# Operands of products 4 and 3 behind products 6 and 4, modulation streams split in turn, put-aside results fetched into the second weight ring

## The chip, the cores and the metric

The kernel runs on one core of a Trainium2 chip. The metric is the time of one execution on the device in microseconds (us). A core has five engines with instruction streams of their own: PE (matrix products), DVE (elementwise on vectors), ACT (elementwise with functions, and casts), POOL (elementwise) and SP (here it issues transfers only). An engine runs its instructions in order, and engines wait for one another by semaphores.

## The reference

One layer of a diffusion transformer over 1024 latent tokens and 256 context tokens of width 1024: a SwiGLU feed-forward half step (hidden width 2816), a mixer (a gated short convolution and attention with 8 query and 2 key heads, merged by gates), a second feed-forward half step and a last norm. Each of the three parts begins with an RMS norm whose result is shifted and scaled, and ends with a gate; shift, scale and gate come from the condition `c` through `w_mod` (1024 x 9216). The functions around which the change turns:

```python
def rms_norm(x, g):
    xf = x.astype(jnp.float32)
    y = xf * lax.rsqrt(jnp.mean(xf * xf, axis=-1, keepdims=True) + EPS)
    return (y * g.astype(jnp.float32)).astype(x.dtype)

def modulate(h, shift, scale):
    return h * (1.0 + scale) + shift

def swiglu(h, w_in, w_out):
    a, b = jnp.split(h @ w_in, 2, axis=-1)
    return (jax.nn.silu(a) * b) @ w_out
...
def conv_branch(bg, cg, vc, conv_w):
    return bg * short_conv(cg * vc, conv_w)
...
def merge_branches(y_conv, o_attn, gate_logits, w_bc, w_ba, w_out):
    g_conv, g_attn = jnp.split(jax.nn.sigmoid(gate_logits), 2, axis=-1)
    return (g_conv * (y_conv @ w_bc) + g_attn * (o_attn @ w_ba)) @ w_out
```

The layer calls `modulate(rms_norm(x, g), shift, scale)` before each part, multiplies by `w_in` (or the mixer's `w_in` of width 6656), and adds `gate * result` to the stream.

## The kernel before

**Arithmetic.** Each fp32 operand is split into a high part, rounded to the matrix engine's fp32r, and a low part, the remainder; a product is three matmuls (high·high, high·low, low·high). `split` does it: the cast to the high part is ACT's, the subtraction for the low part DVE's.

**Products.** The large projections use a Winograd form of the 2 x 2 block product: seven products 1 to 7 instead of eight, for a pair of weight column blocks `(a, b)` of 128 columns each. Left operands are weights or sums of weights (`s1`, `s2`, `s3`, which POOL makes from the raw weights in `lefts`); each is split into a tile `wl` of a ring of four. Right operands are the normed tokens or sums of them, `r1` to `r7`, each in four tiles of 128 rows (k = 0 to 3), made once for a whole projection by `norm0` and `norm1` and kept. A product is four k times three matmuls of 128 x 512. `Winograd.first`, `second` and `third` run the products 1, 2, then 6, 7, 4, then 5, 3, and DVE adds their results in `u`, `c`, `v` and `b`.

**Before the norm of the second half of tokens is there.** Products 1 and 2 need only the first half of the tokens. `start` (lines 664 and following) runs them for the first `n_ahead` pairs while `norm1` makes `r5`, `r6` and at last `r7`, `r4` and `r3` (`late`); it keeps the results `u` and `c` of two pairs on the chip, in a tile `uc` of the ring `wh` (the second weight ring, four slots), and puts those of the others aside in device memory (`put_aside`, tiles `ucd`). `fetch` brings them back, one pair ahead. By the end of `start` all of `norm1` has been run in the program's order (`r7` with the sixth pair, `r4` with the seventh, `r3` with the eighth of nine), so the calls of `late` in `second` find nothing to do. In the first feed-forward the same stands in the loop over `start_together`.

**Rings.** Short-lived tiles (`ttile`) share a pool of eleven slots: `s1` to `s3`, `u`, `c`, `v`, `b`, `y`, the modulation's `rawm` (a loaded piece of `w_mod`), `macc` (its running sums, one for each stream), `acch`, `accl` and `mrow`.

**Modulation.** What is not needed at the start is worked out beside the projections by generators of small steps (`later_mod`): eight steps load a piece of `w_mod` each and add it, times a column of `silu(c)`, to one or two sums on DVE; then the sums are split, PE adds over the partitions, and four small transfers turn the row to columns. `all_later_mods` is run in the first feed-forward's loop, `STEPS[j]` steps at the end of iteration j; m = 6 to 8 (`late_steps`) beside the mixer's projections and the second feed-forward.

**The second matrix of a feed-forward.** `row_products` runs the products in the order 2, 1, 4, 6, 5, 7, 3 over the hidden rows, in groups of two rows. When a product ends, its four banks are added into the stream by DVE (`add`, with the gate), and `after` puts out finished rows or begins the next norm.

**Order.** A scheduler places the instructions of each engine by what they wait for, save those issued while `strict` is set, which keep the order of the program. So the code's order decides only in part, and the rows below are read from the built programs. Line 88 is the helper through which every instruction is issued, so the profile gives it for all of them, and one goes by the tiles' names.

Of the kernel before, what the change touches and what calls it, by code (L numbers as in the profile page):

```python
# [41 lines left out]
STEPS = (0, 4, 4, 4, 5, 5, 5, 5, 5, 5, 5, 2, 12)  # L42
WAIT = 4
# [6 lines left out]
def tile_dit_layer(  # L50
# [211 lines left out]
    def later_mod(m, halves=(0, 1), streams=None):  # L262
# [3 lines left out]
        for half in halves:  # L266
# [12 lines left out]
            for _ in range(WAIT):  # L279
                yield  # L280
            parts = []
            for acc in accs:
                ah, al = ttile("acch", dt=F32R), ttile("accl", dt=F32R)
                split(acc, ah, al)
                parts.append((ah, al))
            for _ in range(6):
                yield
            for (ah, al), v in zip(parts, streams):
                mod, pm = (modl, modc)[v], ps_t()
                matmul(pm[:1], ones_r[:], ah, start=True, stop=False, pinned=True)  # L290
                matmul(pm[:1], ones_r[:], al, start=False, stop=True, pinned=True)
                row = ttile("mrow")
                act.copy(out=row[:1], in_=pm[:1])
                mcol = small("mcol", 4)
                for j in range(4):
                    sp.dma_start(out=mcol[:, j : j + 1], in_=row[:1, j * P : (j + 1) * P])
                c0 = m * 8 + half * 4
                dve.tensor_add(out=mod[:, c0 : c0 + 4], in0=mcol[:], in1=bcol[:, c0 : c0 + 4])
            yield
# [166 lines left out]
    class Winograd:  # L466
# [194 lines left out]
        def start(self, norm):  # L661

            for i in range(self.n_ahead):
                t = wpool.tile([P, 2, 512], F32, tag="wh", name=uniq("uc"), bufs=W_BUFS)
                u, c = t[:, 0], t[:, 1]
                act.copy(out=u, in_=self.product(1))
                run(norm, 2 if i == 0 else 1)
                dve.tensor_add(out=c, in0=u, in1=self.product(2))
                if i < RESIDENT:
                    self.started.append((u, c))  # L670
                else:
                    self.put_aside(t)
            run(norm, 9 - self.n_ahead)
            self.prefetch(4)
            self.late = norm
# [51 lines left out]
        def fetch(self):  # L727

            if self.started and not isinstance(self.started[0], tuple):
                u, c = ttile("u"), ttile("c")  # L730
                for i, t in enumerate((u, c)):
                    load(t, self.started[0][:, i])
                self.started[0] = u, c
# [9 lines left out]
        def second(self, u):  # L743
# [3 lines left out]
            run(self.late, 4)  # L747
# [4 lines left out]
            run(self.late)  # L752
            return v, b

# [40 lines left out]
    def row_products(w, rows, add, after=lambda i, k: None, halves=False):  # L795
# [113 lines left out]
        chain = None  # L909
        for i in (2, 1, 4, 6, 5, 7) + (() if halves else (3,)):  # L910
# [3 lines left out]
            for g, (k, m) in enumerate(groups):  # L914
# [5 lines left out]
                sums(i, g)  # L920
                strict[0] = False
                after(i, k)
            for o, ch in to[i]:
                for d in range(4):
                    add(o + d, ch, ps[d])
            after(i, rows.n)
        if halves:
            kept = []
            ps = [ps_s(256) for _ in range(4)]
            for k, m in groups:  # L930
                for lr in operands(3, k, m):
                    step(3, ps, len(kept), *lr, n=256)
                    kept.append(lr)
                after(8, k)
# [173 lines left out]
    for i in range(7):  # L1108
        if i == 3:
            tx = fetch_tokens(CC)  # L1110
        run(norm1, 1)
# [10 lines left out]
    run(norm1, 1)  # L1122
# [107 lines left out]
    for j in range(NH):  # L1230
        half1.side = side(j) if j >= SIDE_FROM else None
        if j > SIDE_FROM and j % 2:
            raws = context_rows(j)
        u, c = half1.next_first()
        v, b = half1.second(u)
        spill(c, b, j, C0)
        spill(*half1.third(u, v), j, C1)
        run(steps, STEPS[min(j, len(STEPS) - 1)])
        if j == SIDE_FROM - 1:
            for i in range(SIDE_FROM):  # L1240
# [5 lines left out]
                run(steps, 3)  # L1246
# [48 lines left out]
    def after1(i, k):  # L1295
# [23 lines left out]
        if i == 3 and k in (0, 4):  # L1319
# [24 lines left out]
    for i in range(KD):  # L1344
# [4 lines left out]
        if i > 1:  # L1349
            run(late_steps, 5)  # L1350
        for ch, bg, gc in mixed():
            if i > 1:
                run(late_steps, 4)
# [488 lines left out]
    for j in range(NH):  # L1842
        if j > 1:
            run(late_steps, 3)
        u, c = fast.next_first()
        v, b = fast.second(u)
        spill(c, b, j, C0)
        spill(*fast.third(u, v), j, C1)
# [77 lines left out]
```

## Time and profile before

| | us |
|---|---|
| median of 3 runs (lowest to highest) | 2686.76 (2683.47 to 2690.48) |
| the profiled execution's own time | 2688.7 |
| its span | 2686.9 |
| PE busy in it | 2643.4 |
| DVE busy in it | 2007.1 |
| ACT busy in it | 1166.1 |

By time of the span: the first feed-forward's first matrix to about 690 us (from about 277 us the side products of the context tokens stand among it), its second matrix to about 938, the mixer's projections from there to about 1250, attention, the merge, and the second feed-forward from about 2010 to the end. Most windows of 67 us have PE busy throughout. Read such a profile by looking for the windows where it isn't, then for what ended the idle time there, then one engine further back.

### The profile page before, as it was taken

The page shows a single profiled execution, that of the slowest core. Times are in us where ns is not written, and L with a number is a line of the kernel's source. Part 1 is how long each engine was busy: PE and PEld are TensorE (multiplying, and loading weights), DVE is VectorE, ACT ScalarE, POOL GpSimd, SP SyncE. Part 2 cuts the span into 40 slices and gives each one's busy share as a digit, 9 for nine tenths or more (in the row PEclk, how much of TensorE's full clock was granted, in tenths as well). Part 3 has the DMA queues.
Part 4 walks back from the last instruction along what each step waited for, and adds up shares of the span by engine and source line. Part 5 has one row for each costly group of instructions (what it writes and reads, how often), then busy time and mean ns, then how long its engine had stood idle before and what let it go on. Part 6 is the DMA issues. An engine that isn't in the chain of part 4 may idle for free.

```text
span 2686.9 us, 37399 instructions
## 1 busy us (share of the span) xinstructions
PE 2643.4 (98%) x13593; PEld 2236.0 (83%) x13593; DVE 2007.1 (75%) x3356; ACT 1166.1 (43%) x2317; POOL 521.3 (19%) x409
## 2 busy tenths in 40 slices
PE   8999999999999999999999999999999999999998
PEld 5788898888788877888999888877888888888888
DVE  5888888786887889877488666775458875667875
ACT  6633543333454632333244666674236333334543
POOL 1244012121110044232033111000001533230200
PEclk9999999999999999999999999999999999999998
DMA  7655653346973445433213211002524543228731
GB/s 267 236 180 166 223 184 124 109 130 240 293 169 102 149 137 165 134 114 116 97 48 103 95 62 49 24 25 78 167 85 146 184 145 99 83 90 305 165 83 63
DMA packets 369920, 364.84 MB, mean 136 GB/s; under 512 B 27830, under 2 KB 261448, under 8 KB 369736
## 3 DMA queue, kind: packets, MB, share of 16 engines
q1 hardware_dynamic: 360712, 345.17, 39.0%
q0 software_dynamic: 9024, 17.30, 4.0%
q8 instruction: 106, 1.74, 0.3%
q14 instruction: 78, 0.64, 0.1%
HBM read 296.30 MB, written 66.06 MB: 135 GB/s over the span
## 4 chain that ended last, share of the span: by engine, by line
PE 88%; DVE 6%; DMA 2%; ACT 2%; issue 1%; SPq 1%; POOL 0%; DVEq 0%; ACTq 0%; POOLq 0%
PE ps L88 73%; PE po L88 7%; PE pt L88 7%; DMA rawm<-in_w_mod_dram 1%; DVE macc L88 1%; DVE wl L88 1%; SPq L88 1%; DVE xb L88 0%; DVE r L88 0%; ACT r L88 0%; DMA raw<-in_ffn_w_in_dram 0%; DMA xtok<-in_ctx_dram 0%; DVE ol L88 0%; DVE x L88 0%; DVE pts L88 0%
## 5 line engine op out<-in xcount | busy, mean ns | idle before, releaser
L88 PE MATMUL ps<-r,wl 128*128 128x512 f32 x5232 | 1213.4, 392 | 11.6 <-ACT wl L88 6.8
L88 PEld LDWEIGHTS ps<-r,wl 128*128 128x128 f32 x5232 | 983.9, 189 | 220.0 <-ACT wl L88 9.0
L88 ACT CAST wl<-s 128x512 fp32r<-128x512 f32 x256 | 158.0, 620 | 338.3 <-PE ps L88 266.6
L88 POOL TENSOR_TENSOR s<-raw 128x512 f32<-128x512 f32 x64 | 92.4, 1444 | 993.8 <-PE ps L88 346.6
L88 ACT CAST wl<-raw 128x512 fp32r<-128x512 f32 x286 | 176.4, 619 | 250.0 <-PE ps L88 160.6
L88 DVE TENSOR_TENSOR wl<-raw,wl 128x512 fp32r<-128x512 f32 x284 | 202.6, 717 | 68.3 <-ACT wl L88 64.7
L88 DVE TENSOR_TENSOR wl<-s,wl 128x512 fp32r<-128x512 f32 x256 | 231.8, 906 | 12.3 <-ACT wl L88 10.7
L88 POOL TENSOR_TENSOR s<-raw,s 128x512 f32<-128x512 f32 x64 | 99.8, 1560 | 363.9 <-DVE wl L88 354.4
L88 DVE SCALAR_TENSOR_TENSOR macc<-rawm,silu_c,macc 128x512 f32<-128x512 f32 x168 | 137.9, 837 | 9.5 <-DMA rawm<-in_w_mod_dram 9.1
L88 PE MATMUL ps<-wh,r 128*128 128x256 f32 x768 | 141.6, 285 | 0.0
L88 DVE TENSOR_TENSOR pts<-pt,pts 128x512 fp32r<-128x512 f32 x160 | 108.8, 687 | 39.4 <-ACT pts L88 38.4
L88 DVE TENSOR_TENSOR u<-u,ps 128x512 f32<-128x512 f32 x168 | 114.2, 680 | 28.5 <-PE ps L88 28.4
L88 DVE TENSOR_REDUCE m<-ps 128x1 f32<-128x512 f32 (+1 forms) x192 | 110.9, 596 | 31.0 <-PE ps L88 30.3
L88 ACT CAST pts<-pt 128x512 fp32r<-128x512 f32 x160 | 93.2, 593 | 88.7 <-PE pt L88 86.8
L88 ACT CAST rh<-hid 128x512 fp32r<-128x512 f32 x132 | 81.6, 621 | 112.2 <-PE ps L88 96.2
L88 PE MATMUL ps<-rh,wl 128*128 128x512 f32 x360 | 122.0, 389 | 0.0
L88 PEld LDWEIGHTS ps<-wh,r 128*128 128x128 f32 x768 | 120.6, 192 | 0.0
L88 ACT CAST wh<-raw 128x512 fp32r<-128x512 f32 (+1 forms) x88 | 69.3, 795 | 103.0 <-PE ps L88 79.5
L88 PE MATMUL po<-pts,vh 128*128 128x512 f32 x256 | 110.5, 437 | 1.5 <-ACT pts L88 1.5
L88 DVE TENSOR_TENSOR rl<-hid,rh 128x512 fp32r<-128x512 f32 x132 | 90.1, 686 | 26.5 <-ACT rh L88 13.5
L88 PE MATMUL ps<-wl,r 128*128 128x256 f32 x384 | 108.8, 283 | 0.0
L88 PE MATMUL ps<-kl,qs 128*128 128x512 f32 x384 | 105.3, 397 | 0.0
(298 smaller groups left out, 5068.1 us busy)
## 6 DMA issues: line engine op xcount, KB each, us to landing
raw<-in_ffn_w_in_dram SPq DMA_DIRECT2D x125, 512.0 KB
raw<-in_ffn_w_out_dram SPq DMA_DIRECT2D x72, 512.0 KB
rawm<-in_w_mod_dram SPq DMA_DIRECT2D x128, 256.0 KB
raw<-in_w_in_dram SPq DMA_DIRECT2D x61, 512.0 KB
hid<-hd SPq DMA_DIRECT2D x40, 512.0 KB
ws<-in_ffn_w_out_dram POOLq DMA_DIRECT2D x30, 512.0 KB, 6.6
ucd<-uc SPq DMA_DIRECT2D x22, 512.0 KB
hd<-c SPq DMA_DIRECT2D x38, 256.0 KB
```

The lines of the kernel that those rows point to most:

```text
L88: inst = getattr(self.engine, name)(*args, **kw)
```

## The change

It makes five edits. (1) The late operands: `r4` is now made behind product 6 of the first pair and `r3` behind product 4, in the program's order, where both were made in `start`; `r7` stays there, at the last pair but one. (2) A modulation sum is split and added over the partitions one stream after the other, without the waiting steps between, so that half a matrix takes 12 steps in place of 19 (two streams); the steps an iteration are fewer and, in the feed-forwards, spread over it. (3) A fetched pair lands in one tile of the ring `wh`, by one transfer of 512 KB, in place of two tiles of the eleven slots. (4) In `row_products` a product's results are added behind the first group of the next product, in the program's order. (5) The first steps of the mixer's norm stand at groups 2 and 6 of the last product in place of 0 and 4.

```diff
-STEPS = (0, 4, 4, 4, 5, 5, 5, 5, 5, 5, 5, 2, 12)
-WAIT = 4
+STEPS = (0, 3, 3, 3, 3, 3, 3, 4, 4, 4, 4, 1, 8)
...
     def later_mod(m, halves=(0, 1), streams=None):
...
-            for _ in range(WAIT):
-                yield
-            parts = []
-            for acc in accs:
+            for acc, v in zip(accs, streams):
                 ah, al = ttile("acch", dt=F32R), ttile("accl", dt=F32R)
                 split(acc, ah, al)
-                parts.append((ah, al))
-            for _ in range(6):
                 yield
-            for (ah, al), v in zip(parts, streams):
                 mod, pm = (modl, modc)[v], ps_t()
...
                 dve.tensor_add(out=mod[:, c0 : c0 + 4], in0=mcol[:], in1=bcol[:, c0 : c0 + 4])
-            yield
+                yield
...
     def start(self, norm):
...
-                run(norm, 2 if i == 0 else 1)
+                run(norm, 2 if i == 0 else 1 if i < 5 or i == self.n_ahead - 2 else 0)
...
-            run(norm, 9 - self.n_ahead)
             self.prefetch(4)
             self.late = norm
...
     def fetch(self):
 
             if self.started and not isinstance(self.started[0], tuple):
-                u, c = ttile("u"), ttile("c")
-                for i, t in enumerate((u, c)):
-                    load(t, self.started[0][:, i])
-                self.started[0] = u, c
+                t = wpool.tile([P, 2, 512], F32, tag="wh", name=uniq("uc"), bufs=W_BUFS)
+                load(t[:], self.started[0][:])
+                self.started[0] = t[:, 0], t[:, 1]
...
     def second(self, u):
 
             v, b = ttile("v"), ttile("b")
             dve.tensor_add(out=u, in0=u, in1=self.product(6))
-            run(self.late, 4)
+            self.late_operands(1)
             dve.tensor_add(out=v, in0=u, in1=self.product(7))
             if self.side:
                 self.side(0, self.left())
             dve.tensor_sub(out=b, in0=v, in1=self.product(4))
-            run(self.late)
+            self.late_operands()
             return v, b
+
+        def late_operands(self, n=None):
+            strict[0] = True
+            run(self.late, n)
+            strict[0] = False
...
     def row_products(w, rows, add, after=lambda i, k: None, halves=False):
...
-        chain = None
+        chain, results = None, []
+
+        def add_results():
+            while results:
+                i, ps = results.pop()
+                for o, ch in to[i]:
+                    for d in range(4):
+                        add(o + d, ch, ps[d])
+                after(i, rows.n)
...
                 sums(i, g)
+                add_results()
                 strict[0] = False
                 after(i, k)
-            for o, ch in to[i]:
-                for d in range(4):
-                    add(o + d, ch, ps[d])
-            after(i, rows.n)
+            results.append((i, ps))
+        if not halves:
+            add_results()
...
                     kept.append(lr)
+                add_results()
                 after(8, k)
...
     for i in range(7):
         if i == 3:
             tx = fetch_tokens(CC)
-        run(norm1, 1)
+        run(norm1, 1 if i < 4 or i == 6 else 0)
         run(start, 2)
...
     run(start)
-    run(norm1, 1)
     half1.late = norm1
...
+        n_steps = STEPS[min(j, len(STEPS) - 1)]
         u, c = half1.next_first()
+        run(steps, n_steps // 3)
         v, b = half1.second(u)
         spill(c, b, j, C0)
+        run(steps, n_steps // 3)
         spill(*half1.third(u, v), j, C1)
-        run(steps, STEPS[min(j, len(STEPS) - 1)])
+        run(steps, n_steps - n_steps // 3 * 2)
...
-                run(steps, 3)
+                run(steps, 2)
...
-        if i == 3 and k in (0, 4):
+        if i == 3 and k in (2, 6):
             run(norms2, 1)
...
         if i > 1:
-            run(late_steps, 5)
+            run(late_steps, 3)
         for ch, bg, gc in mixed():
             if i > 1:
-                run(late_steps, 4)
+                run(late_steps, 2)
...
     for j in range(NH):
-        if j > 1:
-            run(late_steps, 3)
+        n_steps = j > 1
         u, c = fast.next_first()
+        run(late_steps, n_steps)
         v, b = fast.second(u)
         spill(c, b, j, C0)
+        run(late_steps, n_steps)
         spill(*fast.third(u, v), j, C1)
```

The number of matmuls, sums and casts is the same; SP issues 22 transfers fewer.

ACT at the start of the mixer's projections. `r7`, `r4` and `r3` are right operands, `wl` tiles are weight parts, each made by its cast (the first four `wl` are those of products 6, 7, 4 and 5 of the first pair), `uc` is the result of product 1. Before:

```order
L88 CAST r7_1526_8821<-t34_1511_8756 128x512
L88 CAST r4_1534_8863<-t34_1473_8587 128x512
L88 CAST r4_1535_8866<-t34_1485_8642 128x512
L88 CAST r4_1536_8869<-t34_1498_8699 128x512
L88 COPY uc_1557_8955<-ps_1559_8959 128x512
L88 CAST r4_1537_8872<-t34_1511_8756 128x512
L88 CAST r3_1545_8914<-h12_1472_8586 128x512
L88 CAST r3_1546_8917<-h12_1484_8641 128x512
L88 CAST r3_1547_8920<-h12_1497_8698 128x512
L88 CAST r3_1548_8923<-h12_1510_8755 128x512
L88 CAST wl_1554_8936<-s2_1552_8931 128x512
L88 CAST wl_1558_8956<-s3_1553_8932 128x512
```

and now:

```order
L87 CAST r7_1532_8883<-t34_1503_8740 128x512
L87 COPY uc_1541_8915<-ps_1543_8919 128x512
L87 CAST wl_1538_8896<-s2_1536_8891 128x512
L87 CAST wl_1542_8916<-s3_1537_8892 128x512
L87 CAST wl_1544_8933<-raw_1534_8888 128x512
L87 CAST wl_1547_8952<-s1_1535_8890 128x512
L87 CAST r4_1558_8980<-t34_1465_8571 128x512
L87 CAST r4_1559_8983<-t34_1477_8626 128x512
L87 CAST r4_1560_8986<-t34_1490_8683 128x512
L87 CAST r4_1561_8989<-t34_1503_8740 128x512
L87 CAST wl_1562_8993<-s2_1536_8891 128x512
L87 CAST wl_1569_9020<-s2_1567_9015 128x512
```

The casts of `r4` and `r3` stood ahead of the first weight part; now four weight parts stand ahead of `r4`, and two more ahead of `r3`.

DVE at the end of product 2 of the first feed-forward's second matrix. The `x1` rows add that product's four banks to the stream, `wl` and `wh` are low halves of the weights of product 1 (`wl_1186` is its first before, `wl_1178` now), `rl` low halves of hidden rows, `hid` sums of them. Before:

```order
L88 TENSOR_TENSOR hid_1104_6558<-hid_1105_6559,hid_1104_6558 128x1024
L88 SCALAR_TENSOR_TENSOR x1_1159_6794<-ps_1126_6582,gate1_l_6554,x1_1159_6794 128x512
L88 SCALAR_TENSOR_TENSOR x1_1160_6796<-ps_1127_6583,gate1_l_6554,x1_1160_6796 128x512
L88 SCALAR_TENSOR_TENSOR x1_1161_6798<-ps_1128_6584,gate1_l_6554,x1_1161_6798 128x512
L88 SCALAR_TENSOR_TENSOR x1_1162_6800<-ps_1129_6585,gate1_l_6554,x1_1162_6800 128x512
L88 TENSOR_TENSOR hid_1106_6560<-hid_1106_6560,hid_1104_6558 128x1024
L88 TENSOR_TENSOR rl_1203_7015<-hid_1112_6566,rh_1202_7014 128x512
L88 TENSOR_TENSOR wl_1186_6920<-raw_1185_6918,wl_1186_6920 128x512
L88 TENSOR_TENSOR wh_1189_6941<-raw_1185_6918,wh_1189_6941 128x512
```

and now:

```order
L87 TENSOR_TENSOR rl_1195_6999<-hid_1104_6550,rh_1194_6998 128x512
L87 SCALAR_TENSOR_TENSOR x1_1151_6778<-ps_1118_6566,gate1_l_6538,x1_1151_6778 128x512
L87 SCALAR_TENSOR_TENSOR x1_1152_6780<-ps_1119_6567,gate1_l_6538,x1_1152_6780 128x512
L87 TENSOR_TENSOR wl_1178_6900<-raw_1177_6898,wl_1178_6900 128x512
L87 SCALAR_TENSOR_TENSOR x1_1153_6782<-ps_1120_6568,gate1_l_6538,x1_1153_6782 128x512
L87 SCALAR_TENSOR_TENSOR x1_1154_6784<-ps_1121_6569,gate1_l_6538,x1_1154_6784 128x512
L87 TENSOR_TENSOR wh_1181_6921<-raw_1177_6898,wh_1181_6921 128x512
L87 TENSOR_TENSOR hid_1098_6544<-hid_1098_6544,hid_1096_6542 128x1024
```

The first weight part of product 1 stood behind four `x1` rows, a `hid` and an `rl`; now it stands behind two `x1` rows.

ACT in the first feed-forward, at a fetch. `uc_380` is a fetched tile of the ring `wh`, `c_361` a fetched tile of the eleven slots; the row is its Silu. Before, with the next four weight parts:

```order
L88 ACTIVATE u_313_1574<-u_313_1574 128x512
L88 CAST wl_366_1841<-s2_345_1733 128x512
L88 ACTIVATE c_361_1818<-c_361_1818 128x512
L88 CAST wl_373_1868<-s2_371_1863 128x512
L88 CAST wl_375_1888<-s3_372_1864 128x512
L88 CAST wl_377_1906<-raw_369_1860 128x512
L88 CAST wl_388_1947<-s1_370_1862 128x512
```

and now:

```order
L87 CAST wl_344_1726<-s2_327_1631 128x512
L87 ACTIVATE uc_380_1933<-uc_380_1933 128x512
L87 CAST wl_351_1753<-s2_349_1748 128x512
L87 CAST wl_354_1776<-s3_350_1749 128x512
L87 CAST wl_356_1794<-raw_347_1745 128x512
L87 CAST wl_363_1824<-s1_348_1747 128x512
```

In both a Silu of a fetched tile stands ahead of weight parts. SP, which issues the transfers, has around that fetch now:

```order
L87 DMA raw_347_1745<-in_ffn1_w_in_dram 128x8x128
L87 DMA raw_367_1859<-in_ffn1_w_in_dram 128x8x128
L87 DMA hd_1088<-uc_292_1459 128x512
L87 DMA uc_380_1933<-ucd_184_912 128x1024
L87 DMA rawm_353_1773<-in_w_mod_dram 128x512
L87 DMA rawm_358_1814<-in_w_mod_dram 128x512
L87 DMA rawm_360_1819<-in_w_mod_dram 128x512
L87 DMA hd_1088<-uc_314_1576 128x512
```

The `hd` rows store results; the second store of `uc_292` stands directly ahead of the fetch of `uc_380`, and loads of `w_mod` stand behind it.

## The prediction

> **What bounds the kernel now.** I read the busy shares first, then what PE waited for, then the windows.
>
> ```profile
> span 2686.9 us, 37399 instructions
> PE 2643.4 (98%) x13593; PEld 2236.0 (83%) x13593; DVE 2007.1 (75%) x3356; ACT 1166.1 (43%) x2317; POOL 521.3 (19%) x409
> ```
>
> PE is busy for 2643.4 of 2686.9 us: 43.5 us are idle, and only that, with what a halved clock adds, can be won while PE's work stays as it is. The change adds and removes no matmul. DVE holds 75% on average and is the next engine.
>
> ```profile
> PE ps L88 <- ACT wl L88: 8.0, 4, 5.1
> PE ps L88 <- DVE wl L88: 3.0, 3, 1.8
> ...
> PE pt L88 <- DVE wl L88: 1.7, 1, 1.7
> ...
> PE pt L88 <- ACT wl L88: 1.4, 1, 1.4
> ```
>
> In the view of PE's waits (total, times, longest) the dearest releaser is `wl`, a split weight part: the high half is an ACT cast, the low half a DVE subtraction. 8.0 + 3.0 + 1.7 + 1.4 = 14.1 us over nine waits. The windows say where.
>
> ```profile
> 938.00:1005.00 67.00, 61.95 (x264) 50.70 (x263) 59.42 (x99) 25.76 (x49) 28.15 (x17) 0.95 0.41 134
> 1005.00:1072.00 67.00, 64.43 (x271) 52.39 (x270) 62.45 (x91) 19.14 (x35) 27.32 (x19) 0.95 0.54 172
> 1072.00:1139.00 67.00, 67.00 (x297) 54.99 (x296) 54.75 (x82) 23.80 (x41) 19.08 (x13) 1.00 0.41 126
> 268.00:335.00 67.00, 63.87 (x478) 60.11 (x477) 56.89 (x103) 34.73 (x68) 0.00 (x0) 1.00 0.71 226
> 670.00:737.00 67.00, 63.58 (x293) 52.40 (x293) 59.05 (x84) 31.15 (x53) 8.40 (x7) 1.00 0.95 293
> ```
>
> A row is length, busy time of PE, PEld, DVE, ACT and POOL, then the granted clock (1.00 is full). 1072–1139 is undisturbed: 297 matmuls in 67 us, 0.226 us each, so a product of 12 takes 2.7 us. The four disturbed windows lose 5.05, 2.57, 3.13 and 3.42 us of busy time, and two also lose clock:
>
> ```profile
> 942.40:949.30 6.90, 5.74 (x14) 4.48 (x15) 5.83 (x10) 2.67 (x6) 2.79 (x1) 0.52 0.25 89
> 1058.50:1065.40 6.90, 5.92 (x14) 4.67 (x15) 6.69 (x11) 2.28 (x4) 2.32 (x3) 0.52 0.55 171
> ```
>
> Here PE is busy for 5.74 and 5.92 us at about half the clock, so about 2.9 and 3.0 us are lost beside the idle time.
>
> **Step 1, late operands behind products 6 and 4 (start of the mixers, 938 us).**
>
> ```profile
> 936.17 3.74 ACT L88 CAST r<-t 128x512 fp32r<-128x512 f32 x7
> ...
> 940.82 2.18 ACT L88 CAST r<-h 128x512 fp32r<-128x512 f32 x4
> 942.89 1.14 ACT L88 CAST wl<-s 128x512 fp32r<-128x512 f32 x2
> ...
> 937.93 4.29 DVE L88 TENSOR_TENSOR r<-t,r 128x512 fp32r<-128x512 f32 x7
> ...
> 943.57 6.68 PE L88 MATMUL ps<-r,wl 128*128 128x512 f32 x16 [5.05 <-ACT wl L88]
> ```
>
> ACT writes eight casts of r4 and r3 at about 0.52 us before the first weight part of product 6; DVE does eight subtractions at about 0.6 us (4.29 over 7). The change puts those of r4 behind product 6 and of r3 behind product 4, so the first cast of `wl` comes 8 × 0.52 = 4.2 us earlier, at 938.7, and PE starts 0.68 us later as now, at 939.4: 0.9 us idle in place of 5.05. PE then does four matmuls with high halves (0.9 us) and asks for the low half of product 6, whose subtraction follows r7's four (to 940.3) and the sum of `uc`: ready at 941.6, so 1.3 us more. Behind that, product 3 wants r3, which now stands behind two more weight casts, and the next pair's raw weights; by the same counting about 1.2 us. So 3.4 us of idle time stay of 5.05, and the 2.9 us of clock go if these gaps don't trip the gate again: a gain of 4.5, or 2.8 with one more half-clock window of 3.4 us (cost 1.7). [...] Bounds: 8.0 (all gone) and 0 (the raw weights come no earlier, PE merely waits later).
>
> What trips the gate, the trace shows:
>
> ```profile
> 97.07 0.33 PE L88 MATMUL pt<-ident,xtok 128*128 128x128 f32 x1 [0.61 <-DMA xtok<-in_ctx_dram]
> ...
> 98.94 1.56 PE L88 MATMUL ps<-r,wl 128*128 128x512 f32 x4 [1.32 <-ACT uc L88]
> ...
> 99.40:102.80 3.40, 3.40 (x10) 2.67 (x9) 2.87 (x3) 3.40 (x7) 3.32 (x3) 0.53 0.02 6
> ```
>
> Between 96 and 99.4 us PE stood 0.61 + 1.32 = 1.9 us, and the next 3.4 us ran at half clock. The window 670–737 lost 3.42 us in waits of under 2 us each (the two large ones stand in step 3) and kept 1.00.
>
> [...]
>
> **Step 2, modulation streams in turn, `u` and `c` in the other ring (1055 us).**
>
> ```profile
> 1057.01 0.62 ACT L88 CAST wl<-s 128x512 fp32r<-128x512 f32 x1 [6.41 <-POOL s L88]
> ...
> 1053.04 1.47 POOL L88 TENSOR_TENSOR s<-raw 128x512 f32<-128x512 f32 x1 [10.38 <-DVE accl L88]
> 1055.60 1.37 POOL L88 TENSOR_TENSOR s<-s,raw 128x512 f32<-128x512 f32 x1 [1.09 <-DMA yd<-y]
> ...
> 1057.68 0.73 PE L88 MATMUL ps<-r,wl 128*128 128x512 f32 x2 [1.51 <-ACT wl L88]
> 1059.48 2.07 PE L88 MATMUL ps<-r,wl 128*128 128x512 f32 x4 [1.07 <-DVE wl L88]
> ```
>
> POOL's weight sum waited 10.38 us, and what ended it was the subtraction of `accl`: a slot of the ring of 11 that `s1`, `s2`, `s3`, `u`, `c`, `v`, `b`, `y` and the modulation's tiles share. The second sum waited on the store of a `y`, the same ring. The change takes two of the eleven away for a put-aside pair and splits each stream where it ends, so the waits that held the high and low halves through six further steps are gone. I count the whole stall: 1.51 + 1.07 + 3.0 = **5.5**. Bounds: 0, if another tile of the ring is the last one there, and 5.5.
>
> **Step 3, results added behind the next product's first group (701 us).**
>
> ```profile
> 701.81 2.72 DVE L88 SCALAR_TENSOR_TENSOR x<-ps,gate_l,x 128x512 f32<-128x512 f32 x4
> 702.44 0.62 ACT L88 CAST wl<-raw 128x512 fp32r<-128x512 f32 x1 [0.29 <-DMA raw<-in_ffn_w_out_dram]
> ...
> 703.11 0.50 PE L88 MATMUL pt<-rh,wl 128*128 128x512 f32 x1 [1.39 <-ACT wl L88]
> ...
> 706.18 0.68 DVE L88 TENSOR_TENSOR wl<-raw,wl 128x512 fp32r<-128x512 f32 x1
> ...
> 706.92 0.73 PE L88 MATMUL pt<-rh,wl 128*128 128x512 f32 x2 [1.67 <-DVE wl L88]
> ```
>
> The low half came at 706.18 behind four gated sums (2.72 us), a sum of `hid` and an `rl`. In the new order it stands behind two sums: 703.1, before PE asks for it at 705.2. The 1.67 us go; the 1.39 us end with a load and stay. Gain **1.7**, bounds 0 and 3.1. No other product of this stage shows such a wait, so the same edit there gives nothing.
>
> **Step 4, fewer modulation operations ahead of the side products (277–287 us).**
>
> ```profile
> 272.91 1.14 ACT L88 CAST wo<-raw 128x512 fp32r<-128x512 f32 x2 [5.06 <-DMA raw<-in_ffn_w_out_dram]
> ...
> 277.32 0.39 PE L88 MATMUL ps<-h1ch,wl 128*128 128x256 f32 x1 [1.13 <-ACT wl L88]
> ...
> 285.37 1.41 DVE L88 SCALAR_TENSOR_TENSOR macc<-rawm,silu_c,macc 128x512 f32<-128x512 f32 x2
> 286.69 1.28 DVE L88 TENSOR_TENSOR wl<-raw,wl 128x512 fp32r<-128x512 f32 x2
> 287.43 0.51 PE L88 MATMUL ps<-h1ch,wl 128*128 128x256 f32 x2 [1.80 <-DVE wl L88]
> ```
>
> Fewer steps an iteration (3 for 5) and a share of them earlier in it take the `macc` pairs (1.41 us) from ahead of `wl`; `wo` is loaded earlier, so its casts no longer hold ACT for 5.06 us before the first `wl`. Of 1.13 + 1.80 = 2.9 us I take **2.5**; bounds 0 and 2.9.
>
> **Step 5, the fetch itself and the norms.** Twenty-two transfers of 512 KB replace 44 of 256 KB: the same bytes. The cost is a wait. The ring has four slots, so the fetch can be issued only when the second store of the pair before has landed, and in ACT's order the Silu of the fetched `uc` stands ahead of four weight casts. Something like it is there now:
>
> ```profile
> L88 SPq DMA_DIRECT2D c<-ucd x22: 319/377/486, 151.5 to 2173.8; - x22
> ...
>   ACT c L88: 40.4, 13
> ...
> 200.23 0.42 SPq L88 DMA_DIRECT2D u<-ucd  x1
> ...
> 205.01 0.63 ACT L88 ACTIVATE c<-c 128x512 f32<-128x512 f32 x1 [6.17 <-DMA c<-ucd]
> ```
>
> ACT waited 40.4 us for fetched tiles, 13 times (3.1 us each, once 6.17). PE stood for hardly any of it: of its 8.0 us on ACT's `wl`, 5.05, 1.51 and 1.13 belong to steps 1, 2 and 4, and 0.3 is left. From the first issue (200.23) to the Silu (205.01) are 4.8 us for 512 KB. In the new order the second store is issued about 2.4 us into the next pair (last sum, Silu, product and issue, 0.6 us each); its landing no row shows, so it is put between 0 and the 4.8 of a fetch, at 2.5; the fetch follows with 4.8: the Silu runs 9.7 us after the pair's start. The first cast behind it serves the sixth product, due at 5 × 2.72 = 13.6 us; less 1.3 for cast and subtraction, 2.6 us of slack remain. I charge **1.5** us in all for new small waits; bounds 0 and 22 (a microsecond for each fetch, with a store as slow as 4.8 and a fetch slower by as much as 6.17 − 4.8). The norm's and the broadcast's new places (the last product's groups 2 and 6) leave the counts of ACT and DVE as they are: 0.
>
> **Sum.** 4.2 + 5.5 + 1.7 + 2.5 − 1.5 = 12.4 us. The profiled execution took 2688.7 us (its span 2686.9 and 1.8 around it), 1.9 above the median 2686.8; from the one the changed kernel comes to 2676.3, from the other to 2674.4. I say 2675.
>
> **Rivals.**
> - *The stalls move.* At 938 the wait goes on to the next raw weights and at 1055 to another tile of the ring: steps 1 and 2 give 2 together, steps 3 and 4 their 4.2, less 1.5: 4.7 us, **2683**. For it: the POOL row above waits on two things in turn, so a second one stands behind the first. Against: 1072–1139, with the same code, shows no wait.
> - *The fetch blocks ACT (slower).* Each of 22 fetches comes after the last cast that PE can spare. It decides from 2.6 us beyond the 9.7; every microsecond more costs 22, so from 0.6 us beyond the slack the gain of 13.9 is eaten, and with 1 us the time is 2687 − 14 + 22 = **2695**. For it: ACT and SP work in order, and the new fetch waits on a store that the old one did not share a ring with. Against: the wait of 6.17 us that hid.
> - *Everything goes.* All four at their upper bounds, 8.0 + 5.5 + 3.1 + 2.9 = 19.5: **2667**.
> - *The change does less than it says*, the modulation falling behind and running in one go at the end of a stage: the first stage needs 120 of 139 steps offered, the last 60 of 82, counted in the code, so hardly; it would give the 2683 of the first rival.
>
> **How the numbers follow.** What a measurement of this kernel can tell from no change is about 0.3%, 8 us: 2678.7 is the bound of faster. Forecast (2670 to 2678.7) 0.54; everything goes 0.10; the stalls move, or a part of the gains given back to waits, 0.26; the fetch blocks 0.10. So faster 0.64, same 0.26, slower 0.10; of the last, half lies beyond 2691. The range runs from 2664 (2667 less the 3.3 us by which the fastest run lies under the median) to 2691.
>
> **What would show it.** Step 1 right: PE's longest wait on ACT `wl` at the mixers' start is near 1 us, and the window there has over 64 us busy; wrong if a wait of 3 us or more stands within 20 us behind. Step 2: no POOL sum waits over 5 us on `accl`, clock 1.00 at 1055. Step 3: one wait near 1.4 us at 700, none on DVE `wl`. Step 4: none over 1 us at 270–290. Step 5: waits of ACT on `uc` without a PE wait behind them; if PE waits on `wl` several times between 130 and 270 us or in the last projection, I am wrong on the slower side.

## The result, and the profile after

The changed kernel is **slower**: 2705.28 us, the median of 6 runs (2700.51 to 2714.96), against 2686.66 before (6 runs, 2681.6 to 2690.48). The ratio is 1.0076 with a 95% interval of 1.0056 to 1.0096. Forecast were 2675 and a range of 2664 to 2691.

The page of the profiled execution and the view of PE's waits, as before (total, times, longest):

```profile
span 2702.3 us, 37351 instructions
...
PE 2648.1 (98%) x13593; PEld 2231.7 (83%) x13593; DVE 2034.2 (75%) x3356; ACT 1166.6 (43%) x2317; POOL 534.0 (20%) x409
...
PE ps L87 <- ACT wl L87: 11.6, 9, 2.2
PE ps L87 <- DVE wl L87: 9.3, 12, 1.7
...
PE pt L87 <- DVE wl L87: 0.9, 1, 0.9
```

The single wait of 5.1 us is gone. In its place stand 21 waits of at most 2.2 us on the same `wl`, 20.9 us where there were 11.0. The windows say where, first after and then, for the stages that were not shown, before:

```profile
201.00:268.00 67.00, 60.51 (x252) 46.81 (x252) 58.75 (x86) 19.88 (x39) 24.99 (x16) 0.97 0.49 154
268.00:335.00 67.00, 62.98 (x417) 56.49 (x416) 54.25 (x90) 29.92 (x57) 7.10 (x4) 1.00 0.62 192
335.00:402.00 67.00, 65.68 (x529) 64.13 (x529) 59.65 (x104) 33.15 (x63) 5.79 (x4) 1.00 0.65 205
938.00:1005.00 67.00, 63.35 (x280) 51.07 (x279) 64.76 (x102) 30.51 (x57) 28.55 (x17) 1.00 0.53 171
2077.00:2144.00 67.00, 65.54 (x283) 52.09 (x282) 56.53 (x74) 26.05 (x47) 26.69 (x17) 1.00 0.55 178
2144.00:2211.00 67.00, 63.93 (x278) 51.21 (x277) 59.13 (x75) 18.97 (x33) 29.34 (x19) 1.00 0.49 154
```

```profile
201.00:268.00 67.00, 66.74 (x295) 54.52 (x294) 57.07 (x87) 22.11 (x41) 28.20 (x20) 1.00 0.53 165
2077.00:2144.00 67.00, 67.00 (x297) 55.48 (x296) 57.47 (x79) 23.20 (x39) 30.79 (x20) 1.00 0.59 191
2144.00:2211.00 67.00, 67.00 (x297) 55.25 (x296) 51.85 (x69) 21.14 (x36) 29.41 (x19) 1.00 0.49 155
```

In these windows the first projections of both feed-forwards had next to no wait before (0.26 us of PE's time idle in the first of them); now they have several: 6.49 us of PE's time are idle at 201–268, 3.07 at 2144–2211. For a sum by stage that takes in the half clock as well, I add up, over all matmuls of a trace, how much later the next one starts than is usual (the median) for that shape. It is called the loss below, in us of one profiled execution each. A stretch of 3.4 us at half clock (0.53 at 99.40–102.80 in the kernel before) adds about 1.7 us to it (half its length, an estimate), and almost the same two waits were followed by one in one trace and not in another (last section), so single entries can differ by that much:

| stage (us) | before | after |
|---|---|---|
| 0–67, loads at the start | 11.8 | 14.4 |
| 201–402, first feed-forward, context's part | 5.1 | 17.9 |
| 670–804, its second matrix | 4.2 | 3.1 |
| 938–1005, start of the mixer | 8.1 | 4.7 |
| 1005–1139, mixer | 5.9 | 3.8 |
| 2010–2278, second feed-forward | 0.5 | 7.5 |
| all | 64.1 | 79.8 |

The total rises by 15.7, the span by 15.4. The stages at which gains were forecast do gain, 6.6 us together, except the one at 201–402; what takes it all back is the further loss of 12.8 and 7.0 us in the two loops that fetch. (The first row varies between 10.8 and 14.4 among all the kernels below, and is left out of what follows.)

One turn of the loop, in the timeline after, by engine: DVE, ACT, SP and PE (start, duration, and in brackets the idle time before it and what ended it; `ps` are the banks into which PE writes):

```profile
203.77 0.67 DVE L87 TENSOR_TENSOR uc<-uc,ps 128x512 f32<-128x512 f32 x1
...
206.72 1.78 DVE L87 TENSOR_TENSOR uc<-uc,v 128x512 f32<-128x512 f32 x1
...
204.47 0.63 ACT L87 ACTIVATE uc<-uc 128x512 f32<-128x512 f32 x1 [4.61 <-DVE uc L87]
...
213.83 0.63 ACT L87 ACTIVATE uc<-uc 128x512 f32<-128x512 f32 x1 [8.21 <-DMA uc<-ucd]
214.36 1.12 ACT L87 CAST wl<-s 128x512 fp32r<-128x512 f32 x2
...
208.53 0.34 SPq L87 DMA_DIRECT2D hd<-uc  x1
210.58 0.34 SPq L87 DMA_DIRECT2D uc<-ucd  x1
...
215.02 2.18 PE L87 MATMUL ps<-r,wl 128*128 128x512 f32 x8 [2.19 <-ACT wl L87]
```

The last sum of a pair (203.77), its Silu (204.47) and product (206.72) lead to the store at 208.53; the fetch waits for the store to land and is issued at 210.58; the Silu of what it fetches waits 8.21 us and runs at 213.83; only then come the weight casts, and PE has stood 2.19 us. PE had begun this pair's product 6 at 198.4 and was through with its last product at 212.8 (215.02 − 2.19). And it goes round: late casts make late subtractions and late sums, these a late store, this a late fetch. The fetches stand 16.8 us apart (193.81, 210.58, 227.45), where PE needs 13.6 for a pair (60 matmuls of 0.226).

### The profile page after: what moved, and what is told of

It reads as the page before. It is cut to its first block, busy times and chain, and to the rows that moved or that the text cites. A ratio compares the mean times of both kernels' runs of the same rounds, so it can differ in the third digit from the quotient of the medians.

```text
span 2702.3 us, 37351 instructions
## 1 busy us (share of the span) xinstructions
PE 2648.1 (98%) x13593; PEld 2231.7 (83%) x13593; DVE 2034.2 (75%) x3356; ACT 1166.6 (43%) x2317; POOL 534.0 (20%) x409
## 4 chain that ended last, share of the span: by engine, by line
PE 80%; DVE 8%; DMA 2%; issue 2%; ACT 1%; SPq 0%; DVEq 0%; ACTq 0%
PE ps L87 65%; PE po L87 8%; PE pt L87 7%; DVE wl L87 2%; DVE uc L87 1%; DVE macc L87 1%; DMA rawm<-in_w_mod_dram 1%; DVE nt L87 1%; DMA uc<-ucd 1%; DMA hd<-uc 0%; DVE y L87 0%; DVE v L87 0%; DVE r L87 0%; DVE ol L87 0%; ACT wl L87 0%
## 5 line engine op out<-in xcount | busy, mean ns | idle before, releaser
L87 DVE TENSOR_TENSOR wl<-raw,wl 128x512 fp32r<-128x512 f32 x284 | 199.6, 708 | 66.2 <-ACT wl L87 64.1
L87 DVE SCALAR_TENSOR_TENSOR macc<-rawm,silu_c,macc 128x512 f32<-128x512 f32 x168 | 148.8, 904 | 11.7 <-DMA rawm<-in_w_mod_dram 11.4
L87 POOL TENSOR_TENSOR s<-raw,raw 128x512 f32<-128x512 f32 x64 | 104.6, 1634 | 5.9 <-DVE macc L87 2.9
```

The source lines that it names most:

```text
L87: inst = getattr(self.engine, name)(*args, **kw)
```

## The experiments

Each is a kernel of its own, timed in five rounds against the kernel before on the same chip.

**1. The fetch undone.** From the changed kernel:

```diff
-                t = wpool.tile([P, 2, 512], F32, tag="wh", name=uniq("uc"), bufs=W_BUFS)
-                load(t[:], self.started[0][:])
-                self.started[0] = t[:, 0], t[:, 1]
+                u, c = ttile("u"), ttile("c")
+                for i, t in enumerate((u, c)):
+                    load(t, self.started[0][:, i])
+                self.started[0] = u, c
```

> The changed kernel with one part undone: put-aside results come back as before, two tiles of the eleven slots by two transfers of 256 KB. Theory A (the fetch into the ring of four slots blocks ACT, whose later casts PE then waits for): the windows 201-335 and 2077-2211, which gained 15 and 7.5 us of PE loss over before, go back to before's; ACT's waits on fetched tiles fall from 6 to 8 us each to about 3; about 22 us off the changed kernel's 2705, so 2680 to 2686, below before by what steps 1 to 4 gave (4 to 7 us). Rival B (the modulation's new pacing loads DVE in the loop, the fetch is innocent): 2700 to 2706.

2688.12 us (11 runs), ratio 1.0006 (0.9997 to 1.0014). The fetch is the larger part of the loss: 17 us by the medians. ACT's waits on fetched tiles fall from 60.4 us in all to 22.3, and the loss at 2010–2278 is 0 again. But at 201–402 12.1 us stay, and the kernel is not faster than before: theory A is right on the fetch and wrong on the rest.

**2. The fetch alone**, the same lines put into the kernel before.

> The kernel before with this one part of the change: the fetch into the ring of four slots by one transfer. Theory A: 15 to 25 us slower than before (2702 to 2711), with PE waits of about 2 us on wl between 200 and 290 us. Rival B: 2685 to 2690, same as before. Rival C (it takes both, the fetch and the denser modulation steps, to pass the threshold): between, 2690 to 2698.

2693.4 us (8 runs), ratio 1.0024 (1.0014 to 1.0034): rival C. The loss is 6.9 at 2010–2278, as in the changed kernel, and at 201–402 only 3.6. So the new fetch by itself costs nothing at 201–402. There it costs only beside the modulation's edit: 17.9 with both, 12.1 with the edit and the old fetch (experiment 1).

**3. The Silu tied to `b`.** The changed kernel, in `spill`:

```diff
-        act.activation(out=a, in_=a, func=AF.Silu)
+        z = small("z", 1)
+        dve.tensor_scalar(out=z[:], in0=b[:, :1], scalar1=0.0, scalar2=None, op0=ALU.mult)
+        act.activation(out=a, in_=a, func=AF.Silu, bias=z[:])
```

> The changed kernel with each Silu of the hidden rows given a bias of zero that DVE makes from b, so that it cannot stand in ACT's order ahead of the weight casts before b is there; the fetch stays in the ring of four slots. Theory A1 (what costs is the place of the Silu in ACT's order, not the ring): the waits of PE on wl at 2077-2211 go, those at 201-250 too, those behind the wo casts at 260-300 may stay; 2685 to 2695. Theory A2 (what costs is the ring: slots come back late and everything behind the fetch on SP waits): no better than the changed kernel, 2700 to 2708.

2698.7 us (5 runs), ratio 1.0039 (1.0025 to 1.0053), between the two. The loss at 2010–2278 falls from 7.5 to 3.8; at 201–402 it stays, 19.0.

**4 to 7. The other edits apart**, all with the fetch of before: the late operands, deferred results and the norm's places alone; the modulation's edit alone; the first three with the modulation's edit for m = 6 to 8 only; and experiment 1 with the steps back at the end of an iteration:

```diff
-        n_steps = STEPS[min(j, len(STEPS) - 1)]
         u, c = half1.next_first()
-        run(steps, n_steps // 3)
         v, b = half1.second(u)
         spill(c, b, j, C0)
-        run(steps, n_steps // 3)
         spill(*half1.third(u, v), j, C1)
-        run(steps, n_steps - n_steps // 3 * 2)
+        run(steps, STEPS[min(j, len(STEPS) - 1)])
```

> The kernel before with the late operands behind products 6 and 4, the deferred results and the norm's places only; modulation and fetch as before. Theory D (those edits keep what was forecast of them, 3 to 4 us at 938 and 1 to 2 at 701, and the modulation's new pacing gives them back in the first feed-forward): 2680 to 2684, window 201-335 as in before (5 us of PE loss). Rival E (the late operands themselves bring the loss at 201-335): 2686 to 2692 with over 10 us lost there.

> The kernel before with the modulation's edit alone (streams split in turn, fewer steps, spread over the iteration). Theory D: 5 to 8 us more PE loss at 201-400, 2 to 3 less at 1005-1072: 2689 to 2694. Rival E: 2680 to 2686.

> Late operands, deferred results and norm's places, and the modulation's edit for m of 6 to 8 alone (beside the mixer's projections and the second feed-forward); first feed-forward and fetch as before. Theory D: all the gains together, 2677 to 2682, the fastest so far. Rival E: 2686 or more.

> The kernel with only the fetch undone, and besides the first feed-forward's modulation steps run at the end of each iteration as before, with the new counts and the streams split in turn. If it is the place of the steps within the iteration that costs at 201-335: 2680 to 2684, that loss gone. If it is that each step now holds more work (8 loads in 12 steps for 8 in 19): as with the fetch undone, 2686 to 2690.

| | us (runs) | ratio (95%) | loss 201–402 | mixer's start | 1005–1139 |
|---|---|---|---|---|---|
| 4: late operands, results | 2683.12 (12) | 0.9985 (0.9977 to 0.9994) | 2.9 | 7.1 | 6.4 |
| 5: modulation alone | 2690.79 (11) | 1.0018 (1.001 to 1.0027) | 12.8 | 8.0 | 2.0 |
| 6: 4, and modulation in the mixer | 2680.79 (10) | 0.9981 (0.9972 to 0.999) | 2.7 | 4.6 | 2.6 |
| 7: 1, steps at the end | 2689.27 (11) | 1.0009 (1.0 to 1.0017) | 11.0 | 4.7 | 2.6 |

Theory D holds for 201–402: the modulation's edit brings 6 to 8 us of loss there, and the late operands bring none. The times of 4, 5 and 6 lie in its ranges, that of 7 in the range given for fuller steps. Of the gains that it expects of experiment 4 little is there: the mixer's start loses 7.1 in place of 8.1, and the waits at 701 are those of the kernel before (see step 3 below). The late operands do take the wait of 5.05 us away: it stands unchanged in 5, without them; with them 6 and 7 have two waits of 0.9 and 1.0 us, and 4 has one of 2.67 us. The modulation's edit also brings the gain at 1005. Where in the iteration the steps stand makes little difference (7).

**8 and 9. Lower step counts**, without and with the fetch into the ring:

```diff
-STEPS = (0, 3, 3, 3, 3, 3, 3, 4, 4, 4, 4, 1, 8)
+STEPS = (0, 2, 2, 2, 2, 2, 2, 2, 3, 4, 4, 3, 8)
```

> The kernel with only the fetch undone, and the first feed-forward's step counts lowered from 3 or 4 an iteration to 2 (3 or 4 in iterations 8 to 11), so that the two first half matrices of the modulation and the context's norm end at the same iterations as in the kernel before. Theory F (what costs at 201-402 is that the same work now falls into fewer iterations, and the context's norm into earlier ones): the loss there falls from 12 to about 5 us, 2679 to 2683, as good as the pacing in the mixer alone. Rival G (the split of a stream right behind its sum, or the steps in the middle of an iteration, cost whatever the count): 10 us or more are lost there, 2686 to 2690.

> The whole change, with only those lower step counts. Theory F, with fetch and density hurting by the same queues: the loss at 201-402 falls from 18 to 5 to 8 us; the 7 us of the second feed-forward stay; 2687 to 2694. Rival G: 2700 or more.

8: 2681.91 us (11 runs), ratio 0.9985 (0.9976 to 0.9993), loss at 201–402 5.7. 9: 2692.0 (8 runs), ratio 1.0029 (1.0017 to 1.004), loss there 5.1, and 8.5 at 2010–2278. Theory F holds: one line takes 13 us off the changed kernel, and the loss that the modulation's edit had brought at 201–402 is gone. Theory F has two things in it that these runs don't part: fewer loads an iteration, and the context's norm in later iterations. The traces point to the second for the first waits. In experiment 1 PE waits 1.64 and 0.70 us for `wl` at 247 and 251; from 235 to 252 DVE has 15 operations of that norm (tiles `nt` and `h1cl`) and no modulation sum. In experiment 8 the norm begins only behind 252, as in the kernel before.

**10. Five slots.** The whole change, the ring `wh` with five slots, and 37 for 38 in the large pool.

```diff
-A_BUFS = 38
+A_BUFS = 37
 W_BUFS = 4
+WH_BUFS = 5
...
-                t = wpool.tile([P, 2, 512], F32, tag="wh", name=uniq("uc"), bufs=W_BUFS)
+                t = wpool.tile([P, 2, 512], F32, tag="wh", name=uniq("uc"), bufs=WH_BUFS)
```

> The whole change, with five slots in the second weight ring instead of four (one slot fewer among the 38 of the large pool makes room). If the cost of the fetch is the wait for a slot whose store has to land: ACT's waits on fetched tiles shrink from 60 us in all to under 35, and the loss at 2010-2278 falls from 7.5 to 2 us or less; 2690 to 2697. If it is the transfer itself or the Silu's place, whatever the slots: 2700 to 2707.

2715.78 us (4 runs), ratio 1.011 (1.0096 to 1.0125): a miss. ACT's waits on fetched tiles fell only from 60.4 to 47.1 us, and the loss at 2010–2278 rose to 10.0. In this kernel's timeline at the second feed-forward:

```profile
2145.35 0.34 SPq L88 DMA_DIRECT2D hd<-uc  x1
2147.41 0.34 SPq L88 DMA_DIRECT2D uc<-ucd  x1
...
2150.91 0.63 ACT L88 ACTIVATE uc<-uc 128x512 f32<-128x512 f32 x1 [6.72 <-DMA uc<-ucd]
```

The fetch still stands 2 us behind a store, its Silu behind the fetch. A fifth slot lets the scheduler place the fetch one pair earlier (the last one stands behind the 8th store of a result, in the changed kernel behind the 10th), again where a slot comes free. The two stretches that fetch lose about as much as in the changed kernel, 26.0 us together against 25.4, so one more slot does not take the cost away. The other 15 us of loss are elsewhere, 5.5 of them at 670–804; the smaller large pool may be that, and no run shows it. What is left as a cause is the place of the fetch and of its Silu.

**11 to 14. The place.** With the lower step counts: the fetch kept in the program's order on SP (11); the Silu tied to `b` as in 3 (12); both (13); and the Silu tied, with the fetch of before (14).

```diff
+                strict[0] = True
                 load(t[:], self.started[0][:])
+                strict[0] = False
```

> The whole change with the lower step counts, and each fetch kept in the program's order on SP, so that it stands one pair ahead of its use and not where a slot comes free; the Silu may still follow it directly. Theory H (what costs is that the fetch and its Silu are moved up to the release of a slot, so that each waits for a store that has just been issued): ACT's waits on fetched tiles fall from 56 us to under 20, the loss at 2010-2278 from 8.5 to 2 us or less, 2681 to 2687. Rival I (the place in ACT's order right behind the fetch costs, wherever the fetch stands): 2690 or more.

> The whole change with the lower step counts, the fetch where a slot comes free, and the Silu tied to b by a bias of zero from DVE. Theory H: half of the cost stays, since loads of weights still stand behind the fetch on SP: 3 to 5 us of loss at 2010-2278, 2686 to 2691. Rival I: the loss there is gone, 2680 to 2686.

> Both at once: lower step counts, the fetch in the program's order on SP, and the Silu tied to b. If the two places (SP's and ACT's) are the whole cost of the fetch: no loss over 1 us left at 2010-2278, 2675 to 2679. If something of the ring itself remains: 3 us or more there, 2679 to 2684.

> Lower step counts and Silu tied to b, with the fetch of the kernel before (two tiles of the eleven slots). If the Silu's place cost something with the old fetch too: 2676 to 2680, below the 2681.9 of the same kernel without the tie. If not, as that: 2680 to 2684, and the gain of the tie belongs to the new fetch alone.

| | us (runs) | ratio (95%) | loss 201–402 | 2010–2278 |
|---|---|---|---|---|
| 9: neither | 2692.0 (8) | 1.0029 (1.0017 to 1.004) | 5.1 | 8.5 |
| 11: fetch in order | 2683.58 (11) | 0.9989 (0.998 to 0.9998) | 0 | 6.3 |
| 12: Silu tied | 2680.09 (11) | 0.9975 (0.9966 to 0.9984) | 0.3 | 4.3 |
| 13: both | 2673.7 (5) | 0.995 (0.9936 to 0.9963) | 0 | 0 |
| 14: old fetch, Silu tied | 2678.69 (6) | 0.9968 (0.9956 to 0.9979) | 4.7 | 0 |

In 11 the last fetch of the second feed-forward stands behind the 14th store of a result, in the changed kernel behind the 10th: two pairs later, when it is due. It follows the store at once and no longer waits for it to land; but ACT still waits (53.3 us in all, against under 20 expected by H, whose time alone was right):

```profile
2114.31 0.34 SPq L87 DMA_DIRECT2D hd<-uc  x1
2114.70 0.42 SPq L87 DMA_DIRECT2D uc<-ucd  x1
...
2118.90 0.63 ACT L87 ACTIVATE uc<-uc 128x512 f32<-128x512 f32 x1 [6.47 <-DMA uc<-ucd]
```

In 12 it is the other way round (the loss is that of H, the time that of rival I). ACT waits for no fetched tile; but SP still waits 2 us between store and fetch, the loads of raw weights stand behind it, and POOL's sums wait for these:

```profile
2112.81 0.33 SPq L87 DMA_DIRECT2D hd<-uc  x1
2114.84 0.33 SPq L87 DMA_DIRECT2D uc<-ucd  x1
2116.78 0.38 SPq L87 DMA_DIRECT2D raw<-in_ffn_w_in_dram  x1
...
2121.60 1.29 POOL L87 TENSOR_TENSOR s<-raw 128x512 f32<-128x512 f32 x1 [4.85 <-DMA raw<-in_ffn_w_in_dram]
...
2125.16 16.45 PE L87 MATMUL ps<-r,wl 128*128 128x512 f32 x70 [1.73 <-DVE wl L87]
```

13 has neither, but for one wait of ACT of 5.1 us on a fetched tile, and PE is busy throughout in the windows that had lost most:

```profile
201.00:268.00 67.00, 67.00 (x298) 55.25 (x297) 63.11 (x104) 25.13 (x43) 29.30 (x18) 1.00 0.59 183
268.00:335.00 67.00, 67.00 (x526) 65.27 (x525) 56.82 (x104) 38.14 (x74) 0.00 (x0) 1.00 0.71 222
...
2077.00:2144.00 67.00, 67.00 (x297) 55.21 (x297) 59.78 (x91) 23.98 (x39) 29.37 (x19) 1.00 0.61 188
2144.00:2211.00 67.00, 67.00 (x297) 55.52 (x296) 52.50 (x75) 22.76 (x36) 27.82 (x19) 1.00 0.47 147
```

The two places are the whole cost of the fetch there: loss 8.5 with neither mended, 0 with both, 6.3 and 4.3 with one. 13 takes 5.0 us less than 14 by the medians; since 14 has the old fetch and does not hold it in order either, it is not shown which of the two is worth that. What the tie gives with the old fetch (14 against 8) is not clear of noise: their intervals touch. 13 is the fastest of all, half a per cent below the kernel before.

## Why the prediction was wrong

- **Step 1** (938 us) held in the main: 4.2 us forecast, 3.4 found. Idle times of 0.9 and 1.3 us were worked out for the first two waits; the trace has 0.91 and 1.01:

```profile
954.09 1.25 PE L87 MATMUL ps<-r,wl 128*128 128x512 f32 x4 [0.91 <-ACT wl L87]
956.35 1.89 PE L87 MATMUL ps<-r,wl 128*128 128x512 f32 x7 [1.01 <-DVE wl L87]
```

  The third, 1.2 us at product 3, is not there. Instead PE waits 1.73 us on a low half about 45 us behind the first wait, to 999.36, so the window is 63.35 us busy and not over 64. A wait of 0.7 to 1.9 us at that distance stands in every kernel with the late operands, in none without. That the clock stayed full (1.00 in the row of 938–1005 above) is luck in part: in experiment 1 waits of 0.90 and 1.01 us were followed by 3.4 us at a granted clock of 0.54, and the stage loses 6.7 (last section). No run shows the choice of 4.2, near the 4.5 of full clock; it was an estimate. The stage gained 3.4 us here, with full clock, and 1.4 in experiment 1, with a stretch of half clock.

- **Step 2** (1055 us): no sum on POOL waits for `accl` there any more, but the gain is 2.1 us instead of 5.5; experiments 2 and 5 (3.8 and 2.0 left of 5.9) show that the fetch or the modulation's edit alone brings it. The term was too large since four waits of 0.45 to 0.91 us between 1024 and 1075 came in its place, which the first rival had.
- **Step 3** (701 us): 1.1 instead of 1.7, but not by the mechanism forecast, so the near size is luck. The 1.39 us that were to stay are gone, and of the 1.67 that were to go 0.94 stay. Experiment 4 has the deferred results, and DVE's order and both waits (1.40 and 1.67) are those of the kernel before:

```profile
699.96 2.72 DVE L88 SCALAR_TENSOR_TENSOR x<-ps,gate_l,x 128x512 f32<-128x512 f32 x4
...
701.27 0.50 PE L88 MATMUL pt<-rh,wl 128*128 128x512 f32 x1 [1.40 <-ACT wl L88]
...
704.33 0.69 DVE L88 TENSOR_TENSOR wl<-raw,wl 128x512 fp32r<-128x512 f32 x1
...
705.08 0.73 PE L88 MATMUL pt<-rh,wl 128*128 128x512 f32 x2 [1.67 <-DVE wl L88]
```

  Experiment 5 lacks that edit and has the modulation's, and there `wl` stands behind two sums, with the one wait of the changed kernel:

```profile
712.10 1.40 DVE L87 SCALAR_TENSOR_TENSOR x<-ps,gate_l,x 128x512 f32<-128x512 f32 x2
...
713.42 0.68 DVE L87 TENSOR_TENSOR wl<-raw,wl 128x512 fp32r<-128x512 f32 x1
...
714.15 0.73 PE L87 MATMUL pt<-rh,wl 128*128 128x512 f32 x2 [0.94 <-DVE wl L87]
```

  So the modulation's edit makes the difference here; how it does so is open.
- **Step 4** (277–287 us) is the first of the two failures that made the kernel slower. It reads "Fewer steps an iteration (3 for 5) ... take the `macc` pairs (1.41 us) from ahead of `wl`". The steps were counted, not what is in them. Half a matrix has 8 steps with a load and its sums. They were 8 of 19; they are 8 of 12 with two streams and 8 of 10 with one, as in the two half matrices ahead of the context's norm. Five steps held 2.1 of them, three hold 2.0 to 2.4 and four 2.7 or more; and the context's norm, behind two half matrices, is reached after 20 steps in iteration 7 where it took 38 in iteration 9. In the place of a gain of 2.5 stands a loss of 6 to 8 us (experiments 1, 5, 7), and with the counts lowered it is gone (8: 5.7 against 5.1 before). Which of the two costs, the fuller steps or the earlier norm, is not shown.
- **Step 5**, the fetch, is the second, and the dearer: 1.5 us were charged, 17 measured (the changed kernel against experiment 1; 6.4 in the kernel before, experiment 2, and 10.1 with the lower counts, 9 against 8). Of the rival "the fetch blocks ACT" the mechanism, place and sign were right, and the fetch looked safe because of one term: the second store was put 2.4 us into the next pair, counted from the durations of four instructions with nothing queued ahead of them. In the trace it is issued 10.1 us into it (208.53 against 198.4), behind DVE's other work, so the Silu came at 15.4 us in place of 9.7, past the 13.6 at which PE needs the casts behind it. The landing and the fetch themselves took 2.05 and 3.25 us, 5.3 together, less than the 7.3 assumed. By the rival's own price, 22 us for every microsecond past the slack, these 3.1 us past it would have cost 68; only some of the fetches met the wait. The mixer's fetches cost nothing that shows: its two stages lose 8.5 with the new fetch and 10.0 with the old (experiment 1).
- The rival named SP's order but priced only ACT's. Experiment 12 shows the other half: weight loads on SP stand behind a fetch that waits for a store.
- That these two steps don't simply add is shown by 1, 9 and 8: leaving out the fetch takes off 17 us, lowering the counts 13, both 23. A likely reason is that more work on DVE makes the store late that the fetch waits for; no run tries it by itself.

What stays open besides: why experiment 4 (and 9, 11 and 12) waits 2.6 to 2.8 us at the mixer's start where 6 and 7 wait 1.9 in two parts, and what the five slots cost at 670–804.

## What to carry to other kernels

A tile that is loaded into a ring slot inherits the release of that slot: whatever stands behind the load and behind its first reader, in order, on their engines waits for the last store of the tile that had the slot (here the fetch was issued 2.05 us behind that store, at 210.58, and ACT stood 8.21 us for what it brought). A scheduler that places each instruction as early as its slot allows puts it just there. One slot more did not help here; holding the load and its first reader back to where they are due did (2692.0 to 2673.7 us). When a generator's empty steps are taken out, its work per call goes up and what stands behind it comes earlier, so count the work and not the calls. And when several edits are made at once, a stage that gains as forecast does not show that its edit did it: step 3 needed each edit by itself.

## What the runs showed of the hardware that was not expected

- Almost the same two waits were followed by half clock in one kernel and not in the other. In experiment 1 PE waits 0.90 and 1.01 us between 940.86 and 944.03, and the granted clock behind them is 0.54 for 3.4 us:

```profile
941.40:944.80 3.40, 2.03 (x7) 1.23 (x8) 3.40 (x7) 3.40 (x8) 0.75 (x1) 0.96 0.32 133
944.80:948.20 3.40, 3.40 (x10) 2.67 (x9) 0.98 (x2) 0.55 (x2) 2.12 (x1) 0.54 0.70 223
```

  In the changed kernel it waits 0.91 and 1.01 us between 953.18 and 956.35, and the clock stays:

```profile
951.60:955.00 3.40, 2.49 (x12) 1.56 (x10) 3.40 (x6) 3.40 (x8) 0.00 (x0) 1.00 1.01 353
955.00:958.40 3.40, 2.39 (x11) 1.70 (x10) 3.11 (x6) 2.69 (x6) 2.02 (x1) 1.00 0.53 214
958.40:961.80 3.40, 3.40 (x17) 2.81 (x16) 2.84 (x5) 0.62 (x1) 1.25 (x2) 1.00 0.73 207
```

  So 1.9 us of waits within 3.2 us had half clock behind them in one trace and not in the other; the 1.9 us between 96 and 99.4 in the kernel before, which the prediction shows, had it too (0.53). How long PE waits does not by itself tell whether the clock falls; what else decides, no run tries by itself.

- Some of DVE's operations were longer while POOL ran. Beside POOL's weight sums (204.47 to 209.65) the product of two tiles at 206.72 took 1.78 us; the one at 211.63, with POOL idle, took 0.69; and a sum that reads one of PE's banks (`ps`) took 0.67 beside POOL:

```profile
208.42 0.67 DVE L87 TENSOR_TENSOR uc<-uc,ps 128x512 f32<-128x512 f32 x1
...
211.63 0.69 DVE L87 TENSOR_TENSOR uc<-uc,b 128x512 f32<-128x512 f32 x1
```

  In the whole trace of the changed kernel no such operation that reads a bank took over 0.70 us (112 of `uc<-uc,ps` 0.67 to 0.69); those on two tiles took up to 1.83 (`wl<-s,wl`). The store at 208.53 stands right behind the product at 206.72; with 0.69 us for that product in place of 1.78 it could have been issued about 1.1 us earlier, an estimate from these two rows.
